# Squared ReLU through PSUM, and weight remainders shared by two engines, in both MLPs of a two-layer backbone

## The chip, the core and the metric

The kernel runs on one core of a Trainium2 chip. The metric is the device time of one execution in microseconds (us); a version is represented by the median of its runs. The engines are named as in the profile: PE multiplies matrices, PEld loads its weights, DVE is the vector engine, ACT the scalar (activation) engine, POOL is GpSimd, and SP issues the DMAs. SBUF is the working memory, PSUM the memory in which PE sums its products.

## The reference

Two layers over 128 context tokens and 512 latent tokens (together T = 640 columns), each a mixer and a squared-ReLU MLP, each with an RMSNorm, a shift, a scale and a gate. The change concerns the MLP alone:

```python
def _mlp(h, w1, w2):
    return jnp.square(jax.nn.relu(h @ w1)) @ w2

xp = xp + mp[5] * _mlp(_modulate(_rmsnorm(xp, norm_ff_g[l]), mp[3], mp[4]), w_ff1[l], w_ff2[l])
xs = xs + ms[5] * _mlp(_modulate(_rmsnorm(xs, norm_ff_g[l]), ms[3], ms[4]), w_ff1[l], w_ff2[l])
```

The model width is 1024 and the hidden width 4096. All data are fp32. The mixer of layer 0 is a diagonal state-space model beside a neighbourhood attention; that of layer 1 is a chunked gated DeltaNet.

## The kernel before

**Products in three pieces.** Every fp32 factor is split into a rounded part `hi` and a remainder `lo` (`lo` = the value minus `hi`). A product is hi*hi + hi*lo + lo*hi, three matmuls for each block of 128 rows of the contraction, with 320 columns (half of T) at a time. Splitting a weight takes ACT (the copy that rounds) and then one more engine (the subtraction, called the remainder here).

**The stages of an MLP.** `mlp` goes through four quarters `q` of the hidden width, eight tiles `m` of 128 rows each:

- *First product, plain* (q = 0, six tiles): `gemm`, 24 matmuls for each tile and half. The weights are split by `weight` (L194 on ACT, L196 on POOL). Beside it DVE makes the sums of the quarters of the input that the next form needs (`quarters`, tiles `qt`, `T1` to `T3`, L438 to L461).
- *First product in seven products* (`seven`; one pair of tiles for q = 0, four pairs for q = 1 to 3): two tiles and two halves by Strassen's scheme in Winograd's form. For pair `i` and product `j` (0 to 6), `prep` forms the left factor (L496 to L501 on DVE, sums of weight blocks, tiles `S`, `raw`, `rawx`), rounds it on ACT (L506) and forms its remainder (L507). It runs four products ahead. A product is 12 matmuls (L525 to L527), so a stage of four pairs has 336. The results are added up on DVE (L534 to L550) out of the PSUM bank `p` into `mr` and `msq`.
- *Second product* (`gemm` with `w2`, 384 matmuls): tiles `hidh` and `hidl` against `whi` and `wlo`; DVE adds the result to the residual `x` (L422).

**The squared ReLU** is done by `ev1` after the plain product and by `ev7` after the seven. Each ends in the split of the hidden tile, `hidh` (ACT) and `hidl` (DVE), which the second product reads.

**PSUM** has eight banks, two for each of the tags `pg`, `pa`, `pb` and `pc`. `seven` goes round `pg`, `pa`, `pb`: a bank comes back after six products. The plain `gemm` of the MLP uses `pg` and `pa`: a bank comes back after four products. A bank can be written again when its last reader is done.

**What sets the order.** The code names the operations; a list scheduler with a timeline of its own then sets the order of the instructions on each engine, over the whole program. Each engine works through its list strictly in order. Matmuls of the modulation (L281 to L295, tiles `mraw`, `mrow`, `mtmp`) are put between those of layer 0's MLP.

In the changed kernel, lines from `split` on lie lower: L576 and L577 are there the relu and the square of `ev7`, L572 the square of `ev1`, L567 and L568 the split.

Of the kernel before, what the change touches and what calls it, by code (L numbers as in the profile page):

```python
# [11 lines left out]
F32 = mybir.dt.float32  # L12
F32R = mybir.dt.float32r
I32 = mybir.dt.int32
AF = mybir.ActivationFunctionType
# [5 lines left out]
T = 640          # 128 context tokens, then 512 latent tokens  # L21
HB = 320         # columns of one moving block
# [4 lines left out]
# columns of a half that belong to the context (0) and to the latents (1)  # L27
# [3 lines left out]
# ---------------------------------------------------------------- host: layout only  # L31
# [15 lines left out]
def layout(i):  # L47
# [36 lines left out]
    for d in range(2):  # L84
# [5 lines left out]
        i["state_dn"][0, 0].reshape(2, 4, 2, 128, 128).transpose(1, 3, 0, 2, 4))  # pair, dk, dir, head, dv  # L90
    # S5
    def st(a):  # [2,32,64] -> [64, (d g)]
        return a.reshape(64, 64).T
# [5 lines left out]
    def bm(a):  # [2,32,64,16] -> [64, (d g), 16]  # L99
        return a.reshape(64, 64, 16).transpose(1, 0, 2)  # L100
# [5 lines left out]
         np.concatenate([cr, ci], 0), np.concatenate([ci, cr], 0)], 1))  # [128, 4, 64, 16]  # L106
    # d on the rows 32 i + p of (batch, round): group 8 b + 4 r + i
# [5 lines left out]
    # neighbourhood bias: [pair of heads, query, block kind, head, key]  # L113
# [15 lines left out]
    # constants of the shapes alone  # L129
# [18 lines left out]
# ---------------------------------------------------------------- the kernel  # L148
class Build:
# [9 lines left out]
    def tl(self, shape, tag, dt=F32, bufs=None):  # L159
        """a tile of the phase's pool"""  # L160
        P = self.PA if tag in ("ct", "rt", "L", "s5tmp") else self.P
        return P.tile(shape, dt, name=tag, tag=tag, bufs=bufs or self.BUFS.get(tag, 1))
# [5 lines left out]
    # -------- small helpers  # L168
    def rsqrt(self, pool, a, n, name):
        """1/sqrt(a) on a small tile [128, n] of positive values."""  # L170
# [14 lines left out]
    # -------- weights  # L185
    def weight(self, src, kt=8, j=0):
        """j: its place in a group; two buffers for the first two, one more set for each later one"""
# [11 lines left out]
    def mm_step(self, w, rhs, h, k, kt, p, n, c0=0):  # L199
        """contraction block k of one output tile over one block of columns; rhs: list of (hi, lo)"""  # L200
# [8 lines left out]
    def gemm(self, srcs, rhs, evac, kt=8, lead=1, tail=1, mid=None, after=None, n=HB, tags=("pg",)):  # L209
        """srcs: weight blocks; the first `lead` of them go half by half, the first half block by block,  # L210
        and the last `tail` half by half, with steps of `mid` in between."""
# [31 lines left out]
    # -------- modulation  # L243
# [27 lines left out]
    def mod_half(self, l, nb, kh, P, tag="pc", row=None, dst=None):  # L271
        """Half of the contraction of 256 columns of the modulation."""
# [29 lines left out]
    def mod_scale(self, l, chunk, ni, name):  # L302
        """g * (1 + scale): [128, 8, 2]"""
# [7 lines left out]
    # -------- norms  # L311
# [14 lines left out]
    def rstd_bcast(self, st, tag="pc"):  # L326
        """rows of 1/rms over the columns of a half, in PSUM [128, 320]"""
# [13 lines left out]
    def norm_step(self, h, k, x, bc, a, sh, dst, first=False):  # L341
        """block k of a half; a, sh: [128, 2] scale and shift"""
# [15 lines left out]
    def norm_steps(self, h, x, st, a, sh, dst):  # L358
        """dst: list of 8 (hi, lo) tiles; a, sh: [128, 8, 2] scale and shift"""
# [6 lines left out]
    def start(self, x, dst, P):  # L366
        """the first norm and the start of the input projection, behind the modulation block by block"""
# [48 lines left out]
    def residual(self, x, l, chunk, m, h, p, st):  # L416
        """x[m] += gate * p, and the squares of the sum"""
# [8 lines left out]
    # -------- squared-ReLU MLP  # L426
    # -------- products in 2 x 2 blocks with seven multiplications (Strassen, Winograd's form)
    def quarters(self, hn, pool, tpool):
        """sums of the quarters of hn (halves of the contraction, halves of the columns), split:
        T1 = B12 - B11, T2 = T3 + B11, T3 = B22 - B12, and T2 - B21 in the place of B12"""  # L430
# [38 lines left out]
    def seven(self, srcs, hn, Ts, evac, pool, after):  # L469
        """pairs of output tiles from the quarters"""  # L470
# [18 lines left out]
        def prep(i, j):  # L489
            """the left factor of a product, split"""  # L490
# [16 lines left out]
            nc.gpsimd.tensor_tensor(t[:, 4:8], src, t[:, 0:4], op=SU)  # L507
# [10 lines left out]
        for o, (i, j) in enumerate(order):  # L518
# [16 lines left out]
            elif j == 2:  # L535
                V.tensor_tensor(s1, s1, p, op=AD)
                evac(m, 0, s1)
# [3 lines left out]
            elif j == 4:  # L541
# [3 lines left out]
                evac(m + 1, 1, c)  # L545
            elif j == 5:
                V.tensor_tensor(u3, u3, p, op=SU)
                evac(m + 1, 0, u3)
            else:
                V.tensor_tensor(u2, u2, p, op=AD)  # L550
                evac(m, 1, u2)
                after(i)

    def mlp(self, l, x, hn, st_next, pool, fillers, norm=None, between=(), last=None, tpool=None):
# [8 lines left out]
        for q in range(4):  # L563
            def ev1(m, h, p):
                s = HALVES[h]
                r = pool.tile([128, HB], F32, name="mr", tag="mr", bufs=3)
                nc.scalar.activation(r, p, AF.Relu)  # L567
                sq = pool.tile([128, HB], F32, name="msq", tag="msq", bufs=3)  # L568
                nc.vector.tensor_tensor(sq, r, r, op=ALU.mult)
                nc.scalar.activation(hid[m][0][:, s], sq, AF.Copy)  # L570
                nc.vector.tensor_tensor(hid[m][1][:, s], sq, hid[m][0][:, s], op=ALU.subtract)
            def ev7(m, h, r):  # L572
                nc.scalar.activation(r, r, AF.Relu)
                nc.vector.tensor_tensor(r, r, r, op=ALU.mult)  # L574
                nc.scalar.activation(hid[m][0][:, HALVES[h]], r, AF.Copy)  # L575
                nc.vector.tensor_tensor(hid[m][1][:, HALVES[h]], r, hid[m][0][:, HALVES[h]], op=ALU.subtract)  # L576
            w1 = [self.A["wff1"][l, q * 8 + m] for m in range(8)]  # L577
            if q == 0:
# [14 lines left out]
                self.seven(w1[n:], hn, Ts, lambda m, h, r: ev7(n + m, h, r), pool, filler)  # L593
# [18 lines left out]
    # -------- S5: parameters  # L612
    def s5_params(self, P, sm, ring):
# [28 lines left out]
        def rnd(a, s1, s2=0.0):  # L642
            """round(a * s1 + s2)"""
# [27 lines left out]
        # sine and cosine of phi  # L671
# [26 lines left out]
        # (lam_bar - 1) / lam  # L698
# [23 lines left out]
        # powers of lam_bar: columns k for the forward pairs, 8 - k for the backward ones  # L722
# [25 lines left out]
        # e^{i theta}, theta = 8 phi, and the decay of eight steps  # L748
# [1245 lines left out]
```

## Time and profile before

| | |
|---|---|
| median of 3 runs | 2053.17 us (2051.83 to 2055.7) |
| span of the profiled execution, first to last instruction | 2049.8 us |
| MLP of layer 0 in it | 443.1 to 932.4 us |
| MLP of layer 1 in it | 1555.7 to 2039.3 us |
| busy: PE, PEld | 1818.7 us (89%), 1703.2 us (83%) |
| busy: DVE, POOL, ACT | 1371.1 us (67%), 1004.6 us (49%), 830.1 us (40%) |

The profile lists no time of its own for the profiled execution beyond its span, which is 3.4 us less than the median; the sum of the prediction is made against the span, and the 3.4 us are carried over. Busy is the share of the span in which an engine had an instruction under way. A matmul's record (about 0.31 us) is twice the distance of two starts (about 0.15 us), so a PE that looks busy may still be a little behind; a stage's length against its number of matmuls tells more.

### The profile page before, as it was taken

The page shows a single profiled execution, that of the slowest core. Times are in us where ns is not written, and L with a number is a line of the kernel's source. Part 1 is how long each engine was busy: PE and PEld are TensorE (multiplying, and loading weights), DVE is VectorE, ACT ScalarE, POOL GpSimd, SP SyncE. Part 2 cuts the span into 40 slices and gives each one's busy share as a digit, 9 for nine tenths or more (in the row PEclk, how much of TensorE's full clock was granted, in tenths as well). Part 3 has the DMA queues.
Part 4 walks back from the last instruction along what each step waited for, and adds up shares of the span by engine and source line. Part 5 has one row for each costly group of instructions (what it writes and reads, how often), then busy time and mean ns, then how long its engine had stood idle before and what let it go on. Part 6 is the DMA issues. An engine that isn't in the chain of part 4 may idle for free. (4 is left out here: it accounts for less than half of the span.)

```text
span 2049.8 us, 35800 instructions
## 1 busy us (share of the span) xinstructions
PE 1818.7 (89%) x13476; PEld 1703.2 (83%) x13476; DVE 1371.1 (67%) x2791; ACT 830.1 (40%) x1804; POOL 1004.6 (49%) x821
## 2 busy tenths in 40 slices
PE   5778779999999999998877889798989799999988
PEld 3777757897898989998877888787788799998987
DVE  8877767459457382838679998774558828375563
ACT  4333336444224251535554555354225314243342
POOL 2866635453355454654355545522245526464561
PEclk9989889999999999999998999899989899999999
DMA  8335498524422222332476468768833122222221
GB/s 307 109 112 141 118 279 277 212 99 150 143 80 75 73 83 63 123 113 73 153 219 192 120 195 241 219 176 273 263 125 130 66 73 72 77 72 79 73 91 55
DMA packets 206984, 286.61 MB, mean 140 GB/s; under 512 B 54878, under 2 KB 138236, under 8 KB 206812
## 3 DMA queue, kind: packets, MB, share of 16 engines
q1 hardware_dynamic: 206812, 284.33, 44.2%
q8 instruction: 107, 1.75, 0.4%
q14 instruction: 65, 0.53, 0.1%
HBM read 228.87 MB, written 46.82 MB: 135 GB/s over the span
## 5 line engine op out<-in xcount | busy, mean ns | idle before, releaser
L196 POOL TENSOR_TENSOR wlo<-raw,whi 128x1024 fp32r<-128x1024 f32 (+1 forms) x145 | 341.5, 2357 | 392.1 <-ACT whi L194 384.3
L194 ACT ACTIVATE whi<-raw 128x1024 fp32r<-128x1024 f32 (+1 forms) x153 | 152.8, 999 | 287.5 <-PE pg L206 149.2
L205 PE MATMUL pg<-hidh,whi 128*128 128x320 f32 (+2 forms) x576 | 181.8, 316 | 9.1 <-DVE msq L550 4.6
L207 PE MATMUL pg<-hidh,wlo 128*128 128x320 f32 (+2 forms) x576 | 181.2, 315 | 7.4 <-POOL wlo L196 7.4
L206 PE MATMUL pg<-hidl,whi 128*128 128x320 f32 (+2 forms) x576 | 181.0, 314 | 2.2 <-DVE hidl L576 2.2
L205 PE MATMUL pg<-h10h,whi 128*128 128x320 f32 x472 | 157.6, 334 | 14.8 <-DVE cb L1718 6.4
L422 DVE SCALAR_TENSOR_TENSOR x<-pg,mod,x 128x128 f32<-128x128 f32 (+2 forms) x132 | 53.7, 436 | 172.0 <-PE pg L207 172.0
L207 PE MATMUL pg<-h10h,wlo 128*128 128x320 f32 x472 | 154.4, 327 | 1.2 <-POOL wlo L196 1.2
L206 PE MATMUL pg<-h10l,whi 128*128 128x320 f32 x472 | 154.5, 327 | 0.0
L507 POOL TENSOR_TENSOR wq<-S,wq 128x512 fp32r<-128x512 f32 x78 | 113.5, 1459 | 76.5 <-ACT wq L506 76.5
L205 PE MATMUL pa<-hidh,whi 128*128 128x320 f32 x448 | 138.0, 310 | 0.8 <-ACT whi L194 0.8
L206 PE MATMUL pa<-hidl,whi 128*128 128x320 f32 x448 | 138.3, 309 | 0.0
L207 PE MATMUL pa<-hidh,wlo 128*128 128x320 f32 x448 | 137.6, 309 | 0.0
L422 DVE SCALAR_TENSOR_TENSOR x<-pa,mod,x 128x128 f32<-128x128 f32 (+2 forms) x108 | 43.8, 435 | 130.6 <-PE pa L207 130.6
L205 PEld LDWEIGHTS pg<-hidh,whi 128*128 128x128 f32 x576 | 109.8, 191 | 12.4 <-DVE msq L550 5.3
L207 PEld LDWEIGHTS pg<-hidh,wlo 128*128 128x128 f32 x576 | 110.0, 191 | 9.2 <-POOL wlo L196 9.2
L206 PEld LDWEIGHTS pg<-hidl,whi 128*128 128x128 f32 x576 | 110.1, 191 | 3.3 <-DVE hidl L576 3.3
L205 PEld LDWEIGHTS pg<-h10h,whi 128*128 128x128 f32 x472 | 95.0, 201 | 18.7 <-DVE cb L1718 7.5
L507 POOL TENSOR_TENSOR wq<-raw,wq 128x512 fp32r<-128x512 f32 x56 | 77.0, 1385 | 68.2 <-ACT wq L506 66.0
L1318 DVE SCALAR_TENSOR_TENSOR cv<-cb,cw,cv 128x642 f32<-128x642 f32 x90 | 94.5, 1051 | 10.8 <-ACT cv L1315 9.9
L207 PEld LDWEIGHTS pg<-h10h,wlo 128*128 128x128 f32 x472 | 94.5, 200 | 1.6 <-POOL wlo L196 1.4
L206 PEld LDWEIGHTS pg<-h10l,whi 128*128 128x128 f32 x472 | 94.8, 201 | 0.6 <-issue 0.4
(743 smaller groups left out, 6032.1 us busy)
## 6 DMA issues: line engine op xcount, KB each, us to landing
raw<-in_wff SPq DMA_DIRECT2D x104, 512.0 KB
mraw<-in_wmod SPq DMA_DIRECT2D x96, 512.0 KB
raw<-in_wino SPq DMA_DIRECT2D x33, 512.0 KB
rawx<-in_wff SPq DMA_DIRECT2D x24, 512.0 KB
raw<-in_wine SPq DMA_DIRECT2D x16, 512.0 KB
cka<-pd SPq DMA_DIRECT2D x28, 256.0 KB
ckb<-pd SPq DMA_DIRECT2D x28, 256.0 KB
s5g<-s5g SPq DMA_DIRECT2D x32, 164.0 KB
```

What stands on the lines that cost most here:

```text
L194: nc.scalar.activation(hi[:, :kt], raw[:, :kt], AF.Copy)
L196: (nc.vector if self.lov and self.nw % self.lov else nc.gpsimd).tensor_tensor(lo[:, :kt], raw[:, :kt], hi[:, :kt], op=ALU.subtract)
L205: nc.tensor.matmul(p[:, :n], hi[:, k], xh[:, s], start=(k == 0), stop=False)
L206: nc.tensor.matmul(p[:, :n], hi[:, k], xl[:, s], start=False, stop=False)
L207: nc.tensor.matmul(p[:, :n], lo[:, k], xh[:, s], start=False, stop=(k == kt - 1))
L422: nc.vector.scalar_tensor_tensor(x[m][:, s], p[:, ls], g, x[m][:, s], op0=ALU.mult, op1=ALU.add)
L507: nc.gpsimd.tensor_tensor(t[:, 4:8], src, t[:, 0:4], op=SU)
L1318: V.scalar_tensor_tensor(cv, cb[m][:, t:t + 642], cw[:, t:t + 1], cv, op0=M, op1=AD)
```

## The change

Four things change, all in `seven` and `mlp`; the values that come out are the same sums of the same factors.

- `prep`: the remainder of the left factor goes to DVE for j = 1, 3 and 5 and stays on POOL for j = 0, 2, 4 and 6.
- `ev7` gets the bank `p` as well. The square is no longer `r * r` on DVE, in place in SBUF, but an ACT Square of `r` into `p`.
- `ev1`: the square is no longer `r * r` on DVE into `msq`, but max(p, 0) * r on DVE, in place in the bank.
- In both, the split (`hidh` on ACT, `hidl` on DVE) then reads the bank and no longer an SBUF tile.

```diff
             nc.scalar.activation(t[:, 0:4], src, AF.Copy)
-            nc.gpsimd.tensor_tensor(t[:, 4:8], src, t[:, 0:4], op=SU)
+            (V if j % 2 else nc.gpsimd).tensor_tensor(t[:, 4:8], src, t[:, 0:4], op=SU)
...
                 V.tensor_tensor(s1, s1, p, op=AD)
-                evac(m, 0, s1)
+                evac(m, 0, s1, p)
...
-                evac(m + 1, 1, c)
+                evac(m + 1, 1, c, p)
...
-                evac(m + 1, 0, u3)
+                evac(m + 1, 0, u3, p)
...
-                evac(m, 1, u2)
+                evac(m, 1, u2, p)
...
+            def split(m, h, sq):
+                s = HALVES[h]
+                nc.scalar.activation(hid[m][0][:, s], sq, AF.Copy)
+                nc.vector.tensor_tensor(hid[m][1][:, s], sq, hid[m][0][:, s], op=ALU.subtract)
             def ev1(m, h, p):
-                s = HALVES[h]
                 r = pool.tile([128, HB], F32, name="mr", tag="mr", bufs=3)
                 nc.scalar.activation(r, p, AF.Relu)
-                sq = pool.tile([128, HB], F32, name="msq", tag="msq", bufs=3)
-                nc.vector.tensor_tensor(sq, r, r, op=ALU.mult)
-                nc.scalar.activation(hid[m][0][:, s], sq, AF.Copy)
-                nc.vector.tensor_tensor(hid[m][1][:, s], sq, hid[m][0][:, s], op=ALU.subtract)
-            def ev7(m, h, r):
+                nc.vector.scalar_tensor_tensor(p, p, 0.0, r, op0=ALU.max, op1=ALU.mult)
+                split(m, h, p)
+            def ev7(m, h, r, p):
                 nc.scalar.activation(r, r, AF.Relu)
-                nc.vector.tensor_tensor(r, r, r, op=ALU.mult)
-                nc.scalar.activation(hid[m][0][:, HALVES[h]], r, AF.Copy)
-                nc.vector.tensor_tensor(hid[m][1][:, HALVES[h]], r, hid[m][0][:, HALVES[h]], op=ALU.subtract)
+                nc.scalar.activation(p, r, AF.Square)
+                split(m, h, p)
```

The program as built has 104 more instructions on ACT, 78 fewer on POOL and 26 fewer on DVE (104 squares gone, 78 remainders added). The scheduler's order changes from the start of layer 0's MLP to the end, in layer 1's mixer too, though its operations are the same.

The first place is on DVE, in layer 0, q = 1, around the adding up of the first pair. Before (`mr`, `msq` are the sums, `hidl` the split, `S` and `rawx` the weights' sums of the next pair):

```order
L534 TENSOR_TENSOR msq_6267<-mr_6249,pa_6254 128x320
L496 TENSOR_TENSOR S_6295<-rawx_6293 128x512
L536 TENSOR_TENSOR mr_6249<-mr_6249,pb_6273 128x320
L497 TENSOR_TENSOR S_6295<-S_6295,rawx_6291 128x512
L499 TENSOR_TENSOR rawx_6293<-rawx_6291,rawx_6293 128x512
L574 TENSOR_TENSOR mr_6249<-mr_6249 128x320
L540 TENSOR_TENSOR mr_6312<-msq_6267,pg_6299 128x320
L543 TENSOR_TENSOR msq_6332<-mr_6312,pa_6319 128x320
L544 TENSOR_TENSOR msq_6267<-msq_6267,pa_6319 128x320
L576 TENSOR_TENSOR hidl0_4939<-mr_6249,hidh0_4938 128x320
L501 TENSOR_TENSOR S_6295<-rawx_6291,S_6295 128x512
L574 TENSOR_TENSOR msq_6332<-msq_6332 128x320
```

The same place in the changed program:

```order
L536 TENSOR_TENSOR mr_6237<-mr_6237,pb_6261 128x320
L496 TENSOR_TENSOR S_6283<-rawx_6281 128x512
L497 TENSOR_TENSOR S_6283<-S_6283,rawx_6279 128x512
L499 TENSOR_TENSOR rawx_6281<-rawx_6279,rawx_6281 128x512
L540 TENSOR_TENSOR mr_6300<-msq_6255,pg_6287 128x320
L568 TENSOR_TENSOR hidl0_4939<-pb_6261,hidh0_4938 128x320
L507 TENSOR_TENSOR wq_6304<-S_6283,wq_6304 128x512
L543 TENSOR_TENSOR msq_6320<-mr_6300,pa_6307 128x320
L544 TENSOR_TENSOR msq_6255<-msq_6255,pa_6307 128x320
L501 TENSOR_TENSOR S_6283<-rawx_6279,S_6283 128x512
L547 TENSOR_TENSOR mr_6300<-mr_6300,pb_6330 128x320
L507 TENSOR_TENSOR wq_6349<-rawx_6281,wq_6349 128x512
```

The squares L574 are gone, `hidl0` reads the bank `pb_6261`, and the remainders L507 of the next pair's products 1 and 3 stand behind the sums of products 3 and 5 of this one.

The second place is on DVE too, in layer 1, q = 0, where the first three tiles of the plain product have had their second half multiplied. Before (`qt`, `T1l`, `T3l` are the quarters' sums; the rows are one stretch):

```order
L569 TENSOR_TENSOR msq_17074<-mr_17072 128x320
L453 TENSOR_TENSOR qt_17167<-qt_17167,qt_17168 128x320 x3
L569 TENSOR_TENSOR msq_17105<-mr_17103 128x320
L569 TENSOR_TENSOR msq_17136<-mr_17134 128x320
L460 TENSOR_TENSOR qt_17168<-qt_17167,h13h1_16320 128x320
L571 TENSOR_TENSOR hidl0_16921<-msq_17074,hidh0_16920 128x320
L438 TENSOR_TENSOR T3l_17145<-qt_17167,T3h_17144 128x320
```

In the changed program:

```order
L572 SCALAR_TENSOR_TENSOR pg_17032<-pg_17032,mr_17057 128x320
L460 TENSOR_TENSOR qt_17150<-qt_17149,h13h1_16308 128x320
L460 TENSOR_TENSOR qt_17150<-qt_17149,h13h2_16310 128x320
L572 SCALAR_TENSOR_TENSOR pg_17062<-pg_17062,mr_17087 128x320
L438 TENSOR_TENSOR T3l_17127<-qt_17149,T3h_17126 128x320
L461 TENSOR_TENSOR qt_17150<-qt_17150,h13l1_16309 128x320
L438 TENSOR_TENSOR T1l_17123<-qt_17149,T1h_17122 128x320
L461 TENSOR_TENSOR qt_17150<-qt_17150,h13l2_16311 128x320
L438 TENSOR_TENSOR T3l_17127<-qt_17149,T3h_17126 128x320
L568 TENSOR_TENSOR hidl0_16909<-pg_17032,hidh0_16908 128x320
```

The bank `pg_17032` is now released by the last of these rows, nine instructions behind the square; before, ACT's relu released it.

## Rows read from the trace of the kernel before

**Rows 1.** The page: busy us, share of the span and instructions of each engine

```profile
PE 1818.7 (89%) x13476; PEld 1703.2 (83%) x13476; DVE 1371.1 (67%) x2791; ACT 830.1 (40%) x1804; POOL 1004.6 (49%) x821
```

**Rows 2.** Windows by stage of the MLPs: busy us and instructions, granted clock, DMA

```profile
core 0: us, PE busy (x) PEld busy (x) DVE busy (x) ACT busy (x) POOL busy (x), PEclk, DMA share, GB/s
590.80:648.10 57.30, 53.71 (x358) 52.23 (x356) 48.76 (x72) 28.22 (x57) 35.34 (x26) 0.94 0.26 83
648.10:705.50 57.40, 56.82 (x386) 56.29 (x385) 19.82 (x35) 11.29 (x15) 22.62 (x11) 1.00 0.25 74
...
1555.70:1617.80 62.10, 51.95 (x338) 47.62 (x337) 58.64 (x134) 32.29 (x75) 27.25 (x14) 0.92 0.18 61
...
1633.90:1696.80 62.90, 58.51 (x384) 57.99 (x385) 21.50 (x36) 12.44 (x18) 24.07 (x11) 0.95 0.21 67
1696.80:1749.00 52.20, 50.47 (x338) 49.23 (x336) 43.92 (x64) 27.56 (x56) 35.21 (x25) 1.00 0.26 81
1749.00:1809.00 60.00, 58.24 (x385) 57.98 (x386) 21.39 (x37) 11.86 (x17) 23.89 (x11) 0.97 0.22 71
...
1861.20:1920.20 59.00, 57.07 (x385) 56.55 (x386) 21.12 (x37) 11.81 (x17) 23.92 (x11) 1.00 0.23 72
```

**Rows 3.** What PE waited for in layer 0's MLP: us, times, longest

```profile
PE pc L291 <- DVE mrow L287: 6.5, 3, 3.6
PE pa L527 <- POOL wq L507: 3.2, 4, 0.8
PE pg L207 <- POOL wlo L196: 2.4, 3, 1.6
PE pg L206 <- DVE hidl L576: 2.0, 3, 1.5
PE pc L281 <- DVE mtmp L294: 1.9, 1, 1.9
```

**Rows 4.** What PE waited for in layer 1's MLP: us, times, longest

```profile
PE pa L207 <- POOL wlo L196: 5.9, 1, 5.9
PE pg L207 <- POOL wlo L196: 5.0, 3, 1.8
PE pa L527 <- POOL wq L507: 4.7, 6, 0.8
PE pg L205 <- DVE msq L550: 3.6, 1, 3.6
PE pg L205 <- ACT hidh L575: 2.5, 1, 2.5
```

**Rows 5.** Single lines of DVE: durations ns min/median/max, first and last start

```profile
L574 DVE TENSOR_TENSOR msq<-msq x52: 476/1338/2623, 535.0 to 1979.7; 128x320 f32<-128x320 f32 x52
...
L569 DVE TENSOR_TENSOR msq<-mr x24: 478/481/1360, 474.7 to 1619.1; 128x320 f32<-128x320 f32 x24
...
L534 DVE TENSOR_TENSOR msq<-mr,pa x14: 472/488/489, 526.8 to 1968.8; 128x320 f32<-128x320 f32 x14
...
L497 DVE TENSOR_TENSOR S<-S,raw x14: 677/683/1542, 514.8 to 1942.9; 128x512 f32<-128x512 f32 x14
...
L422 DVE SCALAR_TENSOR_TENSOR x<-pa,mod,x x108: 336/408/553, 394.8 to 1917.6; 128x128 f32<-128x128 f32 x36, 128x192 f32<-128x192 f32 x36, 128x320 f32<-128x320 f32 x36
```

**Rows 6.** Timeline where a second product opens: start us, duration us, engine, line

```profile
1746.15 0.49 DVE L536 TENSOR_TENSOR mr<-mr,pb 128x320 f32<-128x320 f32 x1
...
1747.17 0.49 DVE L574 TENSOR_TENSOR mr<-mr 128x320 f32<-128x320 f32 x1 [0.54 <-ACT mr L573]
...
1747.70 0.47 ACT L575 ACTIVATE hidh<-mr 128x320 fp32r<-128x320 f32 x1 [0.56 <-DVE mr L574]
1748.07 1.04 ACT L194 ACTIVATE whi<-raw 128x1024 fp32r<-128x1024 f32 x1
...
1749.19 2.36 POOL L196 TENSOR_TENSOR wlo<-raw,whi 128x1024 fp32r<-128x1024 f32 x1 [2.40 <-ACT whi L194]
...
1749.63 2.27 DVE L574 TENSOR_TENSOR msq<-msq 128x320 f32<-128x320 f32 x1
```

**Rows 7.** POOL's timeline in layer 1's plain first product

```profile
1599.98 9.52 POOL L196 TENSOR_TENSOR wlo<-raw,whi 128x1024 fp32r<-128x1024 f32 x1 [8.72 <-ACT whi L194]
1609.46 1.53 POOL L507 TENSOR_TENSOR wq<-raw,wq 128x512 fp32r<-128x512 f32 x1
```

**Rows 8.** Window of all between the two MLPs, columns as in rows 2

```profile
932.40:1555.70 623.30, 539.51 (x4649) 502.19 (x4647) 467.81 (x1078) 291.80 (x654) 284.13 (x313) 0.93 0.63 189
```

More of the change, by code (lines that the diff above doesn't have):

```diff
@@ L592, in mlp @@
                     Ts = next(qs)
-                self.seven(w1[n:], hn, Ts, lambda m, h, r: ev7(n + m, h, r), pool, filler)
+                self.seven(w1[n:], hn, Ts, lambda m, h, r, p: ev7(n + m, h, r, p), pool, filler)
             else:
```

## The prediction, made before the changed kernel ran

> **What bounds the kernel now.** I read the page first, then the MLPs stage by stage, then who makes PE wait in them. The page says that PE is busy 89% of the span, and no other engine above 67% [rows 1]. So a faster DVE or POOL is worth only what PE waits for it. The windows give the stages. The second product at 648.10 runs almost without a stop: 57.40 us for 384 matmuls, 149.5 ns each. I take that as PE's pace; a stage of four pairs (336) would then last 50.2 us. The stage at 1696.80 lasts 52.20 us, and four more of the six are within 0.3 us of it; the sixth, at 590.80, lasts 57.30 us. Second products that open worse last 59.00, 60.00 and 62.90 us [rows 2]. So the MLPs, 973 us of the span, hold only some tens of us that another engine could give back.
>
> The waits say which engine. In layer 0 PE waits for DVE (`mrow`, `mtmp`, `hidl`) and for POOL (`wq`, `wlo`); in layer 1 for POOL's `wlo` and `wq`, and for sums and splits that are late [rows 3, 4].
>
> Why they are late can be seen in single instructions. A DVE instruction with two SBUF inputs takes 0.48 us undisturbed, but the square L574 has a median of 1.34 and a longest of 2.62 us. A DVE instruction with one input in PSUM (L534) is never longer than 0.49 [rows 5]. Where a second product opens, the square begins at 1749.63, inside a POOL remainder that ends at 1751.55, and ends 0.35 us behind it. It goes the other way too: a remainder that takes 2.36 us elsewhere takes 9.52 us where DVE issues one two-input instruction after another [rows 6, 7]. I read this as: POOL's instructions and DVE's with two SBUF inputs exclude each other.
>
> In a stage of four pairs this cannot fit. POOL is busy 35.21 us [rows 2]; for each pair DVE has four sums of weights (0.68) and eight squares and splits (0.48), 6.6 us, or 26 a stage [rows 5]. Together that is 61 us in a stage of 52. The overhang builds up until the last pair, where each stage pays two waits of 0.8 us, and runs on into the second product: the sum L536 of the last pair starts only at 1746.15, so `hidh` is ready at 1748.17, `whi` starts behind it in ACT's list, and `wlo`, which PE needs at once, lands at 1751.55 [rows 3, 4, 6].
>
> **The change part by part.** *Remainders.* In 26 pairs 78 of 182 move. POOL keeps four sevenths, 20 us a stage; DVE gets three of 0.68 us a pair (priced as L497, same size and inputs). *Squares of the seven.* 104 leave DVE for ACT, at 0.47 us (an ACT Square into PSUM is in no row; the ACT copies of this size in rows 6 are the nearest; half as much again would not matter, because ACT is busy 27.56 of 52.20 us and would reach 35 to 39 of 50) [rows 2, 6]. *Splits.* `hidl` has one input in PSUM now and no longer excludes POOL. A stage then has 20 us on POOL and 7 x 0.68 x 4 = 19 us of DVE with two SBUF inputs, 39 us of 50: it fits. DVE's own load per pair stays: before 6.6 + 7 x 0.49 = 10.0 us, after 7 x 0.68 + 11 x 0.49 = 10.2 us, of 12.5 that PE takes [rows 5].
>
> What comes back:
>
> - Five stages of four pairs: the two waits of 0.8 us each, 1.6 x 5 = 8 us (bounds 0, and 2.0 each above the floor).
> - The stage at 590.80: 7.1 us above the floor, of which its 20 extra matmuls take up to 3.0; the wait of 3.6 for `mrow` is DVE's backlog. I take 3.5 [rows 2, 3].
> - The openings of the second products, above 57.40: 5.5, 2.6 and 1.6 us in the rows, one more like the last, and in the two with the norm behind them the waits themselves, about 2.0 and 4.3. That is 17.6; some of it is reached only at the half clock that the windows show (0.95, 0.97). In the new order nothing that DVE does ahead of `whi` has two SBUF inputs but the remainders, so I take four fifths, 14 us (bounds 6 and 17.6) [rows 2, 3, 4].
> - Layer 0's other waits for the modulation: 2.9 + 1.9; half of it, 2.5 [rows 3].
>
> *Squares and splits of the plain product.* Here DVE is full: 58.64 of 62.10 us in layer 1 [rows 2]. The square gets the form of L422, 0.55 instead of 0.48, 24 times 0.07, below 2 us in all [rows 5]. What matters more is the bank. ACT's relu released it; now the split does. A bank is wanted again three tiles after its own, some 10.8 us. The second place shown in the order is the worst: three tiles end together, so the fourth bank is wanted one tile (3.6 us) later, but `hidl0` stands nine instructions (4.3 us) behind its square, and the square stands behind two remainders of 2.4 us on POOL. That is up to 9 - 3.6 = 5.4 us of waiting, and some 2 at half clock behind it: 8 us at most. Against it stands the starved remainder: 24 squares and 24 splits no longer shut POOL out, and the wait of 5.9 us can go [rows 4, 7]. I put the two together at 0, bounds -8 and +8.
>
> [...] With one input in PSUM the row has 488 ns, with two in SBUF 481 [rows 5]: nothing to pay for reading the bank. [...]
>
> *The order elsewhere.* Layer 1's mixer has the same work in another order. PE is idle for 623.3 - 539.5 = 83.8 us between the MLPs [rows 8]; a tenth of that is 8.4 us either way, and nothing says which way. I take 0.
>
> Sum: 8 + 3.5 + 14 + 2.5 = 28 us. From the profiled execution's 2049.8 us this gives 2021.8; with the 3.4 us by which the median lies above its span, **2025 us**.
>
> **The rivals.** *Part of it is given back.* The bank waits of the plain products come in both MLPs, or the mixer's new order costs its tenth, or the openings give only 6: 28 - 8 - 8 = 12, or less: 2038 to 2049 us. For it: the waits for the bank stand in the order now. Against: DVE has fewer long instructions ahead of them.
>
> *No change.* What the MLPs gain, the reordered mixer loses: 25 to 30 us of its 83.8 idle us more. 2049 to 2057. Only the extent of the reshuffle speaks for it.
>
> *Slower: DVE becomes the bound of the seven products.* The remainders put more instructions with two SBUF inputs of full size on the engine that waits for POOL. Each pair has seven; each waits w for POOL. DVE needs 10.2 + 7w us a pair, PE 12.5: from w = 0.33 us on, DVE sets the pace. POOL would be busy 40% of the time, and what is left of a remainder of 1.3 us is 0.65 on average: w = 0.26, below the point, though not by much. At w = 0.5 a pair takes 13.7 us, 26 pairs cost 31 us, and the openings keep their waits: about 2080 us. Against it: the durations overlap a little in a full queue, so 10.2 is a high figure, and the remainders have four products, 7 us, until PE needs them.
>
> **How the numbers follow.** The forecast, 15 to 48 us faster (2005 to 2038): 0.72. The upper end of the gain is all bounds together: 10 + 17.6 + 4.1 + 4.8 + 8, with a little of the mixer. Partly given back: 0.12. No change: 0.07. Slower: 0.09. A measurement of this kernel tells 0.2%, 4 us, from no change; so faster 0.84, same 0.07, slower 0.09. The range takes the forecast and the partial case: 2005 to 2047 us.
>
> **What would show it.** In the changed profile the stages of four pairs should last 50 to 51 us, with no PE wait for `wq`; second products 57 to 58 us, with at most one short wait for `wlo`; `hidl` with a longest duration near 0.5 us; POOL 20 us a stage, ACT 35. New PE waits for DVE's split L568 should appear at the start of plain tiles, below 8 us in all. I am wrong if the remainders on DVE have a mean far above 1.1 us and PE waits for them, if `hidl` still lasts as long as POOL's instructions, or if the time between the MLPs moves by more than 10 us.

## The result, and the profile after

The changed kernel takes 2008.03 us (median of 4 runs, 2000.88 to 2011.41), the kernel before 2053.4 in the same comparison: a ratio of 0.9774, 95% interval 0.9761 to 0.9787. That is 45 us faster, where 28 were forecast; the time lies inside the range, near its lower end. The profiled execution has a span of 2005.9 us, 43.9 less than before.

The page of the changed kernel, busy us, share and instructions of each engine (as [rows 1]):

```profile
PE 1808.1 (90%) x13476; PEld 1705.7 (85%) x13476; DVE 1285.6 (64%) x2765; ACT 864.1 (43%) x1908; POOL 894.7 (45%) x743
```

POOL's busy time fell by 110 us, of which 78 remainders at 1.29 us are 101. DVE's fell by 85 although it lost 104 squares of 0.48 us and got 78 remainders of 0.68, 50 against 53: what went there is waiting. The windows by stage of the changed kernel, columns as in [rows 2]:

```profile
443.50:531.20 87.70, 76.38 (x555) 66.27 (x555) 71.83 (x172) 42.16 (x97) 26.90 (x19) 0.92 0.41 142
...
589.50:640.90 51.40, 51.40 (x361) 50.17 (x358) 39.08 (x72) 33.79 (x74) 22.12 (x15) 1.00 0.31 103
640.90:697.20 56.30, 56.30 (x386) 56.30 (x385) 15.60 (x31) 10.89 (x14) 20.11 (x10) 1.00 0.23 75
697.20:746.50 49.30, 49.30 (x338) 49.30 (x338) 36.88 (x65) 34.09 (x74) 22.08 (x15) 1.00 0.26 86
...
913.70:1542.40 628.70, 543.46 (x4667) 505.23 (x4665) 473.37 (x1081) 290.77 (x654) 292.29 (x313) 0.92 0.62 189
1542.40:1619.00 76.60, 65.60 (x406) 61.45 (x406) 68.51 (x152) 41.46 (x94) 26.23 (x18) 0.93 0.16 57
1619.00:1674.80 55.80, 55.80 (x381) 55.80 (x382) 16.20 (x33) 10.87 (x17) 19.85 (x9) 1.00 0.24 76
```

From 1619 us to the end of layer 1's last second product, PE is busy in every window for its whole length. Read at the starts of the stages, with the same windows of the kernel before, the 43.9 us are:

| part of the span, us | before | after | difference | forecast |
|---|---|---|---|---|
| until the first plain product | 443.1 | 443.5 | +0.4 | 0 |
| plain products and the first seven products, layer 0 | 89.1 | 87.7 | -1.4 | -2.5 |
| the same in layer 1 | 78.2 | 76.6 | -1.6 | 0 |
| stage of four pairs at 590.8 | 57.3 | 51.4 | -5.9 | -3.5 |
| the other five stages | 261.8 | 247.1 | -14.7 | -8 |
| eight second products | 486.5 | 460.9 | -25.6 | -14 |
| between the MLPs | 623.3 | 628.7 | +5.4 | 0 |
| after the last second product | 10.5 | 10.0 | -0.5 | 0 |

What PE still waits for in layer 0's MLP of the changed kernel (us, times, longest), the first rows:

```profile
PE pg L205 <- DVE hidl L568: 7.2, 1, 7.2
PE pa L205 <- ACT whi L194: 1.2, 1, 1.2
PE pg L206 <- DVE h03l L352: 1.2, 1, 1.2
PE pc L281 <- DVE mtmp L294: 0.9, 1, 0.9
```

And in layer 1's:

```profile
PE pg L205 <- DVE hidl L568: 3.9, 1, 3.9
PE pc L338 <- DVE nrm_y L182: 2.7, 1, 2.7
PE pa L205 <- ACT whi L194: 1.6, 1, 1.6
PE pb L527 <- DVE wq L507: 0.7, 1, 0.7
```

The waits for POOL's `wq` and almost all for `wlo` of [rows 3, 4] are gone. At the head of both lists stands a new one: `hidl`, the split (line 568) that now releases a bank of the plain products. Single lines of the changed kernel (ns min/median/max, first and last start):

```profile
L568 DVE TENSOR_TENSOR hidl<-pb,hidh x40: 476/484/493, 530.0 to 1936.9; 128x320 fp32r<-128x320 f32 x40
...
L507 POOL TENSOR_TENSOR wq<-S,wq x52: 1286/1296/1762, 515.6 to 1927.4; 128x512 fp32r<-128x512 f32 x52
...
L507 DVE TENSOR_TENSOR wq<-S,wq x26: 672/676/1295, 518.1 to 1920.3; 128x512 fp32r<-128x512 f32 x26
...
L577 ACT ACTIVATE pb<-mr x28: 422/442/443, 528.8 to 1934.8; 128x320 f32<-128x320 f32 x28
```

No split with an input in PSUM takes longer than 0.49 us; the remainders on DVE have a median of 0.68 and a longest in this group of 1.30; ACT's square takes 0.44.

### The profile page after: what moved, and what is told of

Its sections match the earlier page's. It is cut to its first block, busy times and chain, and to the rows that moved or that the text cites. A ratio compares the mean times of both kernels' runs of the same rounds, so it can differ in the third digit from the quotient of the medians.

```text
span 2005.9 us, 35754 instructions
## 1 busy us (share of the span) xinstructions
PE 1808.1 (90%) x13476; PEld 1705.7 (85%) x13476; DVE 1285.6 (64%) x2765; ACT 864.1 (43%) x1908; POOL 894.7 (45%) x743
## 5 line engine op out<-in xcount | busy, mean ns | idle before, releaser
L196 POOL TENSOR_TENSOR wlo<-raw,whi 128x1024 fp32r<-128x1024 f32 (+1 forms) x145 | 335.1, 2313 | 393.9 <-ACT whi L194 378.9
L205 PE MATMUL pg<-h10h,whi 128*128 128x320 f32 x472 | 158.5, 336 | 17.4 <-ACT cb L1312 11.1
L422 DVE SCALAR_TENSOR_TENSOR x<-pa,mod,x 128x128 f32<-128x128 f32 (+2 forms) x108 | 43.9, 435 | 137.2 <-PE pa L207 137.2
L507 POOL TENSOR_TENSOR wq<-S,wq 128x512 fp32r<-128x512 f32 x52 | 70.7, 1360 | 115.6 <-ACT wq L506 115.6
L205 PEld LDWEIGHTS pa<-hidh,whi 128*128 128x128 f32 x448 | 83.9, 188 | 4.4 <-ACT whi L194 3.6
```

What stands on the lines that cost most here:

```text
L196: (nc.vector if self.lov and self.nw % self.lov else nc.gpsimd).tensor_tensor(lo[:, :kt], raw[:, :kt], hi[:, :kt], op=ALU.subtract)
L205: nc.tensor.matmul(p[:, :n], hi[:, k], xh[:, s], start=(k == 0), stop=False)
L422: nc.vector.scalar_tensor_tensor(x[m][:, s], p[:, ls], g, x[m][:, s], op0=ALU.mult, op1=ALU.add)
L507: (V if j % 2 else nc.gpsimd).tensor_tensor(t[:, 4:8], src, t[:, 0:4], op=SU)
```

## The experiments

The changed kernel is the base of all. Its three parts can be undone apart: the remainders (in `prep`), the square and split of the seven products (`ev7`), and those of the plain products (`ev1`).

### One part alone

**Remainders alone** (`ev1` and `ev7` as before; the edit of `ev7` is shown, that of `ev1` stands under "The change without its `ev1`"):

```diff
 def ev7(m, h, r, p):
     nc.scalar.activation(r, r, AF.Relu)
-    nc.scalar.activation(p, r, AF.Square)
-    split(m, h, p)
+    nc.vector.tensor_tensor(r, r, r, op=ALU.mult)
+    split(m, h, r)
```

> Only the remainders move (three of seven to VectorE); squares and splits as in the kernel before. Theory (POOL's instructions and DVE's with two SBUF inputs exclude each other): a stage of four pairs has 20 us on POOL and 4 x (7 x 0.68 + 8 x 0.48) = 34 us of such instructions on DVE, 54 us for a floor of 49.4: it still does not fit, DVE's squares still have durations above 1 us, stages stay at 50 to 52 us and second products at 57 to 60; in all 2030 to 2045 us. Rival (POOL was late only because seven remainders a pair were too many for it): POOL has half its load, stages fall to 49.4 and second products to 56.3 to 57; 2003 to 2018 us.

Measured: 2016.97 us, ratio 0.9831 (0.9803 to 0.9858): inside the rival's forecast and 13 us below the theory's, which missed. A stage of four pairs and the second product behind it, windows of this run:

```profile
1676.20:1725.50 49.30, 49.30 (x339) 49.30 (x338) 45.34 (x77) 28.20 (x57) 20.94 (x15) 1.00 0.26 86
1725.50:1783.50 58.00, 56.86 (x386) 56.33 (x386) 21.06 (x36) 11.28 (x15) 21.47 (x10) 1.00 0.23 73
```

The stages are as short as in the changed kernel, as the rival had it; the second products keep 1.7 us of their late opening, as the theory said, and DVE's squares still last up to 2.63 us. So time and stages speak for the rival and the openings for the theory; the run after this one decides. The timeline of this one (start us, duration us, engine, line) shows the exclusion and what was wrong in the count:

```profile
1704.18 0.48 DVE L578 TENSOR_TENSOR mr<-mr 128x320 f32<-128x320 f32 x1
...
1704.36 1.46 POOL L507 TENSOR_TENSOR wq<-S,wq 128x512 fp32r<-128x512 f32 x1 [2.45 <-ACT wq L506]
1704.59 1.58 DVE L568 TENSOR_TENSOR hidl<-msq,hidh 128x320 fp32r<-128x320 f32 x1
...
1706.49 0.48 DVE L568 TENSOR_TENSOR hidl<-mr,hidh 128x320 fp32r<-128x320 f32 x1
...
1706.90 0.68 DVE L507 TENSOR_TENSOR wq<-raw,wq 128x512 fp32r<-128x512 f32 x1
...
1707.50 0.48 DVE L568 TENSOR_TENSOR hidl<-msq,hidh 128x320 fp32r<-128x320 f32 x1
```

The split at 1704.59 meets a remainder on POOL that ends at 1705.82, and itself ends 0.35 us later. But in a full queue the next instruction starts 0.40 us after one of 320 columns and 0.60 after one of 512 (1706.49, 1706.90, 1707.50). The durations of 0.48 and 0.68 overlap, so the 54 us of the theory are 28 x 0.60 + 32 x 0.40 + 16 x 1.27 = 50 us, for a stage of 49.3: nearly a fit.

**The seven products' square alone** (`prep` and `ev1` as before; the edit of `prep` is shown):

```diff
-(V if j % 2 else nc.gpsimd).tensor_tensor(t[:, 4:8], src, t[:, 0:4], op=SU)
+nc.gpsimd.tensor_tensor(t[:, 4:8], src, t[:, 0:4], op=SU)
```

> Only the square and the split of the seven products change (ACT squares into PSUM, DVE splits from there); all seven remainders stay on POOL. Theory (exclusion): a stage has 35 us on POOL and 4 x 4 x 0.68 = 11 us of DVE with two SBUF inputs, 46 us for 49.4: it fits by a little, stages 49.4 to 50.2, second products 56.3 to 57.5, in all 2005 to 2020 us; the remainders on DVE would then be worth almost nothing. Rival (POOL's number of remainders): the two waits of 0.8 us for wq stay, stages 51.5 to 52.2, and the openings keep their waits for wlo: 2030 us or more.

Measured: 2012.1 us, ratio 0.9802 (0.9777 to 0.9828), as the theory has it. Windows of the same two places:

```profile
1675.50:1724.80 49.30, 49.30 (x339) 49.30 (x338) 32.03 (x54) 34.76 (x74) 35.22 (x26) 1.00 0.26 86
1724.80:1781.10 56.30, 56.30 (x386) 56.30 (x385) 14.96 (x30) 10.88 (x14) 21.84 (x11) 1.00 0.23 76
```

POOL is as busy as before, 35.22 us, and PE waits for it nowhere in the stage or the opening. In these stages the number of remainders on POOL was not the cause.

That the remainders on DVE would then be worth almost nothing was a miss. With both (the run without `ev1`, below) the time is 1990.96 us, 21 us less than here. Of the 15.0 us between the two profiled spans 12.7 lie between the end of layer 0's MLP and the end of layer 1's first second product. There PE waits longest, in this run, for POOL in the plain products:

```profile
PE pa L207 <- POOL wlo L196: 5.8, 1, 5.8
```

This wait and one of 1.6 us for `wlo` in the opening are 2.2 and 0.2 us in the run with both: 5 us of the 12.7. The rest is not explained by these runs.

**The plain products' square alone** (`prep` and `ev7` as before, both edits as shown above).

> Only the square of the plain products changes (in place in PSUM, split from there); the seven products as in the kernel before. Theory (the bank is held until the split): one wait of PE for DVE's hidl of 3 to 8 us in each plain part, the parts 1 to 7 us longer than the 60.7 and 62.2 us of before, stages of four pairs 52.0 as before; 2045 to 2062 us, the rest by the order between the MLPs. Rival (the starved remainders of POOL weigh more): plain parts 3 to 6 us shorter, 2038 to 2048 us.

Measured: 2045.64 us, ratio 0.996 (0.9945 to 0.9974), a time that both forecasts allow. PE waits for `hidl` 7.2 us in layer 0 and 4.3 in layer 1, as the theory said. The plain products take 66.8 us in layer 0, 6 more than before, but 61.6 in layer 1, not more than before; with the first seven products behind them it is the other way round, 86.2 (89.1 before) and 80.7 (78.2). So the lengths were half missed. Stages of four pairs stay at 52. The profiled execution (2053.09) is the slowest of the ten, and says little on where the 8 us come from.

### Does the memory of the square matter, or only that it left DVE?

The run with the seven products' square alone, and one edit: ACT writes the square into SBUF.

```diff
-    nc.scalar.activation(p, r, AF.Square)
-    split(m, h, p)
+    nc.scalar.activation(r, r, AF.Square)
+    split(m, h, r)
```

> As the run with the seven products' squares alone changed (remainders on POOL), but ACT writes the square into SBUF, so DVE's split has two SBUF inputs again; the plain products as in the kernel before. Nothing but the place of the square differs between the two runs. Theory (exclusion, an instruction of 320 columns shutting POOL out for the 0.40 us from its start to the next one's, one of 512 for 0.60): a stage has 28 x 1.27 us on POOL and 16 x 0.60 + 16 x 0.40 us of such instructions on DVE, 51.6 us for 49.4, where the other run had 45.2: it does not fit by 2 us, so the splits have longest durations above 1 us again and the second products open with waits of 1 to 3 us (57.5 to 59.5 us instead of 56.5); 2016 to 2028 us. Rival (what counted was that the squares left DVE, in whichever memory they land): stages 49.4, second products 56.5, 2006 to 2014 us.

Measured: 2026.23 us, ratio 0.9871 (0.9852 to 0.9891), 14 us slower than with the square in PSUM. Windows of this run, a stage and the second product behind it:

```profile
1679.40:1729.80 50.40, 49.95 (x338) 49.23 (x336) 39.39 (x52) 32.86 (x70) 33.78 (x25) 1.00 0.25 84
1729.80:1788.10 58.30, 56.68 (x384) 56.42 (x385) 18.80 (x33) 13.10 (x19) 23.96 (x11) 1.00 0.23 73
```

Half of the seven products' splits of this run, among its single lines (ns min/median/max), and below them one of the three groups of the run with the square in PSUM:

```profile
L568 DVE TENSOR_TENSOR hidl<-mr,hidh x52: 478/1335/2460, 530.3 to 1952.3; 128x320 fp32r<-128x320 f32 x52
...
L568 DVE TENSOR_TENSOR hidl<-pb,hidh x40: 474/491/494, 528.5 to 1937.7; 128x320 fp32r<-128x320 f32 x40
```

The same instruction on the same engine has a median of 1.34 us in this group with its input in SBUF and 0.49 with it in PSUM. (The other splits from SBUF, `msq`, have a median of 0.485 and a longest of 2.34; none of the 104 from PSUM is longer than 0.494.) The opening's 2 us are back. Only the memory differs, so the second SBUF input is what costs; that POOL is what it waits for shows in the timeline above and in the run with all remainders on DVE, below. Together they show the exclusion, for these shapes.

With 1.27 us for a remainder on POOL (its shortest in the run with the seven's square alone) and 0.60 and 0.40 for DVE's, what a stage needs in turns stands so against what was measured (second product: the one after it):

| kernel | POOL x 1.27 | DVE x 0.60 | DVE x 0.40 | sum, us | stage | second product |
|---|---|---|---|---|---|---|
| before | 28 | 16 | 32 | 58 | 52.3 | 58.8 |
| square by ACT into SBUF | 28 | 16 | 16 | 52 | 50.4 | 58.3 |
| remainders alone | 16 | 28 | 32 | 50 | 49.3 | 58.0 |
| seven's square alone | 28 | 16 | 0 | 45 | 49.3 | 56.3 |
| changed | 16 | 28 | 0 | 37 | 49.3 | 56.3 |

The three sums above 49.3 are the three kernels whose second products open late. One of them, remainders alone, has a stage as short as the others, so the sum tells to a microsecond or two, not better, where lateness begins.

### What does the held bank cost?

**The change without its `ev1`:**

```diff
-    nc.vector.scalar_tensor_tensor(p, p, 0.0, r, op0=ALU.max, op1=ALU.mult)
-    split(m, h, p)
+    sq = pool.tile([128, HB], F32, name="msq", tag="msq", bufs=3)
+    nc.vector.tensor_tensor(sq, r, r, op=ALU.mult)
+    split(m, h, sq)
```

> The change without the part on the plain products (their square has two SBUF inputs again, and ACT's relu releases the bank). Theory (the 7.2 and 3.9 us that PE waited for hidl in the changed kernel are the price of the held bank): no such wait, plain parts 4 to 8 us shorter than the changed kernel's 66.8 and 60.2 us, stages 49.4 as there; 1995 to 2004 us. Rival (what is given up, POOL no longer shut out by the squares, is worth as much): POOL's wlo is starved again, with one wait of 4 to 6 us in layer 1; 2003 to 2012 us.

Measured: 1990.96 us, ratio 0.9695 (0.967 to 0.972): 17 us faster than the changed kernel, more than either forecast allowed. Its windows of the plain parts and of the time between the MLPs:

```profile
442.80:527.00 84.20, 77.31 (x577) 63.78 (x578) 73.02 (x175) 42.28 (x97) 28.57 (x19) 0.98 0.46 157
...
907.50:1530.20 622.70, 548.37 (x4668) 511.67 (x4666) 466.05 (x1081) 289.91 (x654) 279.64 (x313) 0.91 0.63 190
1530.20:1605.10 74.90, 64.23 (x406) 59.95 (x406) 70.56 (x152) 41.92 (x94) 32.45 (x18) 0.95 0.17 57
```

The wait for `hidl` is gone, and the plain products take 60.6 and 56.0 us instead of 66.8 and 60.2, as the theory said. Of the 13.8 us by which its span (1992.1) is shorter, 3.5 lie in layer 0's plain part (with the first seven products), 6.0 between the MLPs, 1.7 in layer 1's plain part and 2.0 later in layer 0. There the changed kernel runs some 20 matmuls of the modulation that this run has in its plain part (577 there against 555). The granted clock of layer 0's plain part is 0.98, where the changed kernel has 0.92.

**The square of the plain products by ACT, into PSUM** (bank held, 24 instructions less on DVE):

```diff
-    nc.vector.scalar_tensor_tensor(p, p, 0.0, r, op0=ALU.max, op1=ALU.mult)
+    nc.scalar.activation(p, r, AF.Square)
```

> The changed kernel, with the plain products' square by ACT into PSUM as in the seven products; the bank is still held until DVE's split, DVE has 24 instructions less. Theory (the held bank is the price): PE still waits for DVE's hidl, once in each plain part, 2 to 7 us; 1996 to 2008 us. Rival (it was the square's place in DVE's queue, not the bank): the waits go, plain parts 60 and 56 us; 1985 to 1993 us.

**The same into SBUF** (bank released by the relu):

```diff
-    nc.vector.scalar_tensor_tensor(p, p, 0.0, r, op0=ALU.max, op1=ALU.mult)
-    split(m, h, p)
+    nc.scalar.activation(r, r, AF.Square)
+    split(m, h, r)
```

> The changed kernel, with the plain products' square by ACT into SBUF: ACT's relu releases the bank, DVE has 24 instructions less, its splits have two SBUF inputs. Theory (the held bank is the price, and DVE is full in the plain parts): no wait for hidl, plain parts at most 60.7 and 56.1 us; 1982 to 1992 us. Rival (splits from SBUF are starved by POOL there, and hidh late): plain parts as in the changed kernel, 1998 us or more.

Measured: into PSUM 1997.13 us (ratio 0.9726, 0.9705 to 0.9747), into SBUF 1997.81 (0.9733, 0.9712 to 0.9753). What PE waited for in layer 0's plain part, the first row of the run into PSUM:

```profile
PE pg L205 <- DVE hidl L568: 7.2, 1, 7.2
```

And of the run into SBUF:

```profile
PE pc L291 <- DVE mrow L287: 3.3, 1, 3.3
```

So the wait for `hidl` belongs to the held bank, whoever makes the square. But the 7.2 us are not what holding it costs the kernel: with ACT's square the two runs, with the bank held and without, take the same time. This is a net figure, because without the bank the split has two SBUF inputs again, and what that costs is not measured apart. The windows of layer 0's plain part, into PSUM and into SBUF:

```profile
443.20:526.90 83.70, 74.91 (x556) 65.09 (x556) 67.88 (x158) 47.05 (x109) 26.14 (x18) 0.94 0.41 144
...
443.10:524.30 81.20, 74.75 (x555) 63.46 (x555) 66.31 (x159) 47.26 (x109) 27.73 (x19) 0.98 0.45 151
```

With as many matmuls, the part with the wait of 7.2 us is 2.5 us longer. (The run without `ev1` takes 84.2, but for 577 matmuls.) The run into SBUF, forecast at 1982 to 1992, missed: its plain products take 61.6 and 59.1 us where at most 60.7 and 56.1 were forecast, it has 626.2 us between the MLPs, 1.4 more than the run into PSUM and 3.5 more than the run without `ev1`, and no gain in layer 1's plain part (75.1).

In the changed kernel and in the run into PSUM the bank is held alike, and only the engine of the plain products' square differs: 2008.03 against 1997.13 us. So 11 of the 17 us go with DVE's in-place square. The 6 us that are left, from both runs with ACT's square to the run without `ev1` (1990.96), are not explained by these runs.

**The new square of the plain products in one layer only** (layer 0 shown; the other run has `l == 1`):

```diff
+    if l == 0:
         nc.vector.scalar_tensor_tensor(p, p, 0.0, r, op0=ALU.max, op1=ALU.mult)
+        sq = p
+    else:
+        sq = pool.tile([128, HB], F32, name="msq", tag="msq", bufs=3)
+        nc.vector.tensor_tensor(sq, r, r, op=ALU.mult)
-    split(m, h, p)
+    split(m, h, sq)
```

> The changed kernel, with the new square of the plain products in layer 0 alone (layer 1's as in the kernel before). The order between the MLPs is then that of the changed kernel. Theory (of what the new square costs the change, some 17 us, most comes with layer 0: its held bank, and an order of the mixer that is some 6 us longer): wait of 7.2 us for hidl in layer 0, none in layer 1, between the MLPs 626 to 631 us; 2002 to 2008 us. Rival (the cost is that of the two waits, and the order does not matter): between the MLPs as in the run with plain products as before, 622 to 624; 1995 to 2000 us.

> The changed kernel, with the new square of the plain products in layer 1 alone (layer 0's as in the kernel before). The order between the MLPs is then that of the run with plain products as before. Theory: wait of some 4 us for hidl in layer 1 alone, of which 1 to 2 us remain in the plain part; between the MLPs 622 to 624 us; 1991 to 1996 us. Rival (layer 1's wait costs as much as layer 0's, or the time between the MLPs does not go with the order): 1998 us or more.

Measured: layer 0 alone 2006.59 us (ratio 0.9774, 0.9748 to 0.9801), layer 1 alone 1989.1 (0.9686, 0.9664 to 0.9708). The windows between the MLPs and of layer 1's plain part, in the run with layer 0:

```profile
908.70:1533.90 625.20, 537.77 (x4669) 502.13 (x4666) 474.92 (x1081) 290.61 (x654) 291.38 (x313) 0.93 0.62 190
1533.90:1611.80 77.90, 66.14 (x406) 62.77 (x406) 71.02 (x153) 41.60 (x95) 37.30 (x19) 0.91 0.17 56
```

The same two windows in the run with layer 1:

```profile
906.10:1526.70 620.60, 546.31 (x4667) 510.01 (x4665) 467.74 (x1080) 290.15 (x654) 279.64 (x313) 0.92 0.63 191
1526.70:1600.40 73.70, 62.77 (x409) 58.17 (x406) 69.28 (x152) 42.13 (x94) 26.54 (x18) 0.98 0.16 58
```

The whole cost comes with the edit in layer 0: in layer 1 it costs nothing, though PE waits 2.9 us for the bank there. The run with layer 1 took less than was forecast, in all (1991 to 1996) and between the MLPs (622 to 624). The split of layer 0's cost stays open: the profiled execution with layer 0 alone (2000.56) is the fastest of that kernel's four (up to 2009.67), and there the time between the MLPs is 3.5 us shorter than in the changed kernel's, below the 626 that were forecast. Its layer 1, which has the old square, takes 77.9 us for the plain part, 3.0 more than in the run without `ev1`, with a wait of 4.2 us for POOL's `wq` that the other has at 0.4: the scheduler's order behind the edit changes too, and no run holds it fixed.

### All remainders on DVE

Base: the run without `ev1`.

```diff
-(V if j % 2 else nc.gpsimd).tensor_tensor(t[:, 4:8], src, t[:, 0:4], op=SU)
+V.tensor_tensor(t[:, 4:8], src, t[:, 0:4], op=SU)
```

> As the run with remainders and seven squares (plain products as before), but all seven remainders of a pair on DVE. Theory (the exclusion costs DVE nothing when POOL has nothing there, and an instruction takes DVE 0.40 or 0.60 us from start to start): DVE needs 4 x 11 x (0.60 + 0.40) = 44 us in a stage of 49.4, stages and second products as with three on DVE (49.4, 56.5), the plain parts 0 to 6 us longer because DVE is full there; 1988 to 2000 us. Rival (the slower case of the prediction: DVE sets the pace of the seven products): PE waits for wq of DVE in the stages, these 51 us or more; 2005 us or more.

Measured: 1998.88 us, ratio 0.9738 (0.9717 to 0.9759). A window of a stage:

```profile
691.10:740.40 49.30, 49.30 (x338) 49.30 (x337) 40.96 (x79) 34.99 (x74) 2.10 (x1) 1.00 0.28 86
```

The largest group of its remainders, among the single lines:

```profile
L507 DVE TENSOR_TENSOR wq<-S,wq x78: 674/681/693, 516.2 to 1916.5; 128x512 fp32r<-128x512 f32 x78
```

DVE is busy 41 of 49.3 us and PE runs without a stop. Even seven remainders a pair don't make DVE the bound of the stage, and with POOL almost idle none is ever longer than 0.69 us. The weights' sums with two SBUF inputs show the other side: where POOL has its share of the remainders, in the changed kernel, line 497 has medians of 1.47 and 1.67 us, for 0.68 undisturbed [rows 5]. The plain parts are not longer, as was allowed for, but shorter (83.3 and 74.0); the run is still 8 us slower by medians than with three on DVE, of which its profile shows only 2.5 (625.2 us between the MLPs against 622.7).

## Why the prediction was right, and where its sizes were off

**The mechanism was right.** The exclusion holds (memory of the square, above), POOL is busy 22 us a stage (20 forecast) and ACT 34 (35), the split's longest duration is 0.49 us, no remainder makes PE wait in a stage of four pairs. DVE's remainders cost what [rows 5] gave for a sum of that size.

**PE's pace was mis-sized, and this is most of the difference of 17 us.** The step that was off is the floor. The prediction took the second product at 648.10 [rows 2] as running "almost without a stop": 57.40 us, 149.5 ns a matmul, 50.2 for a stage. Its waits in the kernel before, in that window:

```profile
PE pg L207 <- POOL wlo L196: 0.3, 1, 0.3
PE pg L206 <- DVE hidl L576: 0.2, 1, 0.2
```

A wait listed at 0.3 costs PE more than that, as the starts around the first one show, in the kernel before (start us, duration us, engine, line):

```profile
648.50 0.31 PE L206 MATMUL pa<-hidl,whi 128*128 128x320 f32 x1
649.15 0.41 PE L207 MATMUL pg<-hidh,wlo 128*128 128x320 f32 x1 [0.35 <-POOL wlo L196]
649.40 0.31 PE L205 MATMUL pg<-hidh,whi 128*128 128x320 f32 x1
```

Two steps from start to start take 0.90 us here and 0.29 elsewhere in this stage: 0.6 us lost; around the second wait it is 0.5. Without waits the second product is now 56.30 us, 1.1 less. PE's pace is 56.3 / 384 = 49.3 / 336 = 147 ns. Six stages at 0.9 and eight second products at 1.1 us make 14.2 us, of the 20.7 by which stages and second products came out better than forecast. The other 6.5 are the shares that were taken below the bounds: four fifths of the openings, 1.6 us for two waits of 0.8 where up to 2.0 were open, 3.5 of the 7.1 us of the stage at 590.80.

**The openings**: that nearly all of their waits go was right; of `wlo` and `whi` waits are left in the first opening of each layer alone, 0.4 and 1.2 us in layer 0, 0.2 and 1.6 in layer 1. The half clock that the prediction saw in the opening windows can be read there: in the kernel before, behind the wait of 1.6 us that ends at 1751.61, the granted clock is 0.50 from 1752.70 to 1755.50 us, and the matmuls start 0.27 us apart instead of 0.147. In the changed kernel every window from 1619 to 1995.9 us has 1.00.

**Plain products and modulation** gave 3.0 us, forecast 2.5 + 0. But the new waits are 11.1 us together, where "below 8" was forecast, and the longer is in layer 0, where the prediction looked at layer 1. The timeline of the changed kernel shows how it comes about (start us, duration us, engine, line):

```profile
467.69 4.67 POOL L196 TENSOR_TENSOR wlo<-raw,whi 128x1024 fp32r<-128x1024 f32 x2 [4.13 <-ACT whi L194]
...
468.00 2.07 DVE L295 TENSOR_TENSOR mod<-mtmp,bmod 128x4 f32<-128x4 f32 x1
...
468.90 0.42 ACT L571 ACTIVATE mr<-pg 128x320 f32<-128x320 f32 x1
...
470.08 2.62 DVE L451 TENSOR_TENSOR qt<-h03h 128x320 f32<-128x320 f32 x1
...
475.11 0.48 DVE L572 SCALAR_TENSOR_TENSOR pg<-pg,mr 128x320 f32<-128x320 f32 x1
...
477.51 0.48 DVE L568 TENSOR_TENSOR hidl<-pg,hidh 128x320 fp32r<-128x320 f32 x1
```

ACT's relu has read the bank at 469.3; before, that released it. Now the square waits until 475.11 behind a tiny `mod` and a sum of the quarters, each held up by a `wlo` on POOL (0.15 us and 0.48 elsewhere in the same queue), and behind seven more instructions; the split stands six instructions further. Behind the wait the granted clock is 0.50 from 478.0 to 483.8 us: 20 steps of 0.27 us instead of 0.147, by estimate 2.4 us, where the prediction put some 2 behind its wait in layer 1. Even so the part lost less than the wait, as the runs on the held bank show.

**The order elsewhere** was put at 0 with 8.4 either way, and gave back 5.4: inside its bounds, its cause not settled. Every run with the old square in layer 0's plain products and three remainders on DVE has 620.6 to 626.8 us there, the runs with DVE's in-place square in layer 0 625.2 to 633.5. The two overlap, and the run with the seven products' square alone, old square and all, has 628.1, so that square does not decide it by itself.

**The rivals.** "Partly given back" was right in its two places (bank and mixer), but the gain around them was larger than it allowed. "Slower" asked for 0.33 us of waiting for each of the seven instructions of a pair with two SBUF inputs and 512 columns. The three remainders wait little (a mean of 0.74 us, for 0.68 undisturbed), but the four sums of weights do wait: all 182 take 163.8 us in the changed kernel, 0.90 each, so w was 0.22, near the 0.26 that the rival reckoned with. It did not bind all the same, because the count of 10.2 us a pair took durations where starts lie 0.40 and 0.60 us apart: DVE is busy 36.9 us of a stage, 9.2 a pair of 12.3, waits included.

**Luck.** Stages and second products together gave 46.2 us, where the bounds of the prediction came to 31.7. The time lies inside the range none the less because other parts gave less than their bounds allowed: plain products and modulation 3.0 of 12.8 us, and the order between the MLPs took 5.4.

**Reading PSUM** was priced at nothing, and the runs bear it out for this instruction: splits from PSUM have medians of 0.480 to 0.484 us in the changed kernel and 0.490 to 0.491 in the run with the seven products' square alone, undisturbed ones from SBUF 0.478 (the plain products' in that run): at most 13 ns more.

## What to carry to other kernels

Where VectorE and GpSimd share the work of a stage, add up in one sum GpSimd's time and that of VectorE's instructions with two SBUF inputs, counted from start to start. Where this sum came out above the stage (50, 52 and 58 us for 49.3), what followed the stage opened late here, and an operand in PSUM helped without any work being moved to another engine: 14 us between two kernels that differ only in the memory of the square.

A bank that holds an intermediate is held until its last reader is done, and PE waited 7.2 us for one here. But such a wait is not a price by itself: with ACT's square, keeping the intermediate in the bank or in SBUF made no difference to the time. Why the new square costs 16 to 19 us in layer 0 is not shown, beyond that 11 us go when ACT makes it. So try such a move in each place by itself: the kernel that has it in the seven products and not in the plain ones (1991 us, or 1989 with layer 1's plain products changed as well) beats the one that has it everywhere (2008).

And a floor read from the best stage of a trace still has that stage's small waits in it; the starts of undisturbed instructions give the pace without them.

## What the runs showed of the hardware

ACT's instructions of 128x320 were shorter here with one side in PSUM. By medians in the changed kernel, the relu took 0.461 to 0.472 us from SBUF into SBUF (line 576) and 0.424 to 0.430 from PSUM into SBUF (line 571); the copy from PSUM into SBUF 0.420 to 0.437 (line 567), where the kernel before has 0.472 to 0.473 from SBUF into SBUF (lines 570 and 575). The square from SBUF into PSUM took 0.435 to 0.442 (line 577).

A DVE instruction of four columns took 2.07 us beside POOL's `wlo` (the `mod` above, 0.15 us elsewhere): it started 0.31 us behind the first of two `wlo`, 4.67 us together, and ended at 470.07, where the first `wlo` ends at about 470.0 if the two took the same time. So the wait was for POOL's instruction, however little DVE had to do.
